# Experts of a MoE block: transposes and bias products gathered into two groups per expert

## The chip, the cores and the metric

The kernel runs on one core of a Trainium2 chip. The metric is the device time of one execution in microseconds (us). All times below are of that one core.

## The reference

A decoder block: an S5 branch and a gated MLP branch side by side, merged, then a mixture of 32 experts of which each token takes four, then a last norm. Only the mixture matters here (512 tokens of width 1024, float32):

```python
logits = tok @ router_w + router_b
top_val, top_idx = lax.top_k(logits, 4)
weights = jax.nn.softmax(top_val, axis=-1)
...
def expert_block(args):
    rows, e = args
    xb = tok[rows]
    gu = xb @ w_in[e] + b_in[e]                 # 1024 -> 2048
    gate, up = gu[:, :1024], gu[:, 1024:]
    gate = jnp.minimum(gate, 7.0)
    up = jnp.clip(up, -7.0, 7.0)
    act = (up + 1) * (gate * jax.nn.sigmoid(1.702 * gate))
    return act @ w_out[e] + b_out[e]            # 1024 -> 1024
...
out = zeros.at[row_tok].add(row_weight * expert rows)
```

## The kernel before, in words

The front part (the two branches, the router and the tables of tokens per expert) takes the first 430 us or so and is not changed. Then `expert` runs 32 times, unrolled, e0 to e31.

Every expert has a main part of up to 64 tokens. POOL gathers their rows into `xab[e % 3]`, two half rows to a partition, by an indirect DMA that is issued two experts ahead. Experts with more than 64 tokens run further blocks under `tc.If`: a `single` block (`c_up`, `c_down`; tiles `xc`, `actc`, `pc`) and a `pair` block (`ab_up`, `ab_out` with `pc` tiles). On this input 12 experts have the single block (e4, 6, 9, 12, 13, 16, 18, 22, 25, 27, 28, 30) and 6 the pair block (e11, 12, 17, 22, 26, 27); 17 have neither, and PE branches past the code of both. In the order of the program a single block stands under an If ahead of the main up (L1400), a pair block under one behind it (L1402), and their second halves under two Ifs behind the main up (L1411, L1413).

The weights stay in float32. SyncE (SP) loads them by `prefetch` as tiles of 1 MB, eight `wi` and four `wo` for an expert, into a ring of 19 tiles; a tile is asked for when the one that held its place has been read.

On the main path of an expert, PE (TensorE) does:

- two bias products into the PSUM tiles `pu` (`biased`, L1287): `sel` (which expert's bias goes to which row) times `bhl`;
- `ab_up` (L1293, products at L1300): 32 products, 8 K tiles by 2 halves u by 2 column groups g. K tiles 0 to 3 run for both halves, then 4 to 7 for u = 0, then 4 to 7 for u = 1. A product of float32 is two MATMUL instructions, so a K tile of one half is four in the profile, and a main up is 64;
- between those, after K tile 3, `start(e + 1)`: PE transposes the next expert's rows (`transposed`, L1264, into the PSUM tile `pt`), ACT moves them to SBUF scaled in eight pieces (L1270), DVE makes its `sel`;
- `swiglu` on each half `pu`: DVE g and u, ACT a sigmoid, DVE a product and `act` (L1278 to L1282);
- `ab_out` (L1312): transposes of `act` of half 0 (copied to `aab` by ACT at L1272), two bias products into `pd`, then `ab_down` (L1309), 16 products, four of them ahead of the transposes of half 1, twelve behind. DVE scales the result to `yab`, POOL adds it to the output by an indirect DMA.

PE's order is the order of the Python code (`tc.manual_schedule(engines={ET.PE})`); on DVE, ACT, POOL and SP a scheduler places the instructions. The pool of `pt` has two buffers; `pu` (two tiles) and `pd` have one each.

Of the kernel before, what the change touches and what calls it, by code (L numbers as in the profile page):

```python
# [9 lines left out]
F32 = mybir.dt.float32  # L10
# [18 lines left out]
NE, TOPK, DE = 32, 4, 1024  # L29
# [12 lines left out]
def tile_hybrid_block(ctx: ExitStack, tc: tile.TileContext, x, c, ada_w, ada_b, norm1_g, w_in,  # L42
# [20 lines left out]
    def H(shape, dt=F32, name="h"):  # L63
        return big.tile(shape, dt, tag="H", name=name)
# [63 lines left out]
    for i in range(2):  # L128
        t = H([128, 2, 1024], name="xt")
# [324 lines left out]
    pu = product(hT, True, evac_u, raw_in[0])  # L454
# [396 lines left out]
    aT = [(ahi[:, k], alo[:, k]) for k in range(4)]  # L851
# [62 lines left out]
    for i in range(2):  # L914
        t = H([128, 2, 1024], name="x2")
# [211 lines left out]
    xT, pps = {}, {}  # L1127
# [48 lines left out]
    tab0, tabp = [rt.tile([128, 1, 32, 3], I32, name=m) for m in ("tab0", "tabp")]  # L1176
# [44 lines left out]
    xab = [rt.tile([128, 512], F32, name=f"xab{a}") for a in range(3)]  # L1221
# [6 lines left out]
    pab = ctx.enter_context(tc.tile_pool(name="pab", bufs=1, space=PS, reuse_waits="tile"))  # L1228
# [22 lines left out]
    def gather_more(e):  # L1251

        x_ = xce[e % 3]
        with tc.If(single[e] > 0):
            gather(x_[:, 512:768], hrow4, tab1[:, 0, e, 0:1], 4)
        with tc.If(pair[e] > 0):
            gather(x_[:, 0:512], hrow2, tabp[:, 0, e, 0:1], 2)

    def transposed(src, n, tag, bufs, scaled=False):


        ps = PT()
# [12 lines left out]
    def swiglu(p, act):

        g, u, sg = [mo.tile([128, 256], F32, tag=t, bufs=1, name=t) for t in ("g", "u", "s")]
        v.tensor_scalar(g, p[:, 0:256], LIMIT, None, op0=OP.min)  # L1278
        sc.activation(sg, g, AF.Sigmoid, scale=ALPHA)  # L1279
        v.tensor_scalar(u, p[:, 256:512], -LIMIT, LIMIT, op0=OP.max, op1=OP.min)  # L1280
        v.tensor_mul(g, g, sg)
        v.scalar_tensor_tensor(act, u, 1.0, g, op0=OP.add, op1=OP.mult)  # L1282
        return act

    def biased(o, s_, n, cols_, first=True):

        return pe.matmul(o, s_, bhl[:, n, cols_], start=first, stop=False)  # L1287

    def acts(n, tag):
        return [mo.tile([128, 256], F32, tag=tag, bufs=n, name="act") for _ in range(n)]  # L1290


    def ab_up(xT, wi, sel, n, p, between=None):  # L1293
        for u in range(2):
            biased(p[u], sel[:, 1 + u], n, slice(0, 512))
        for k, u in [(k, u) for k in range(4) for u in range(2)] + [(k, u) for u in range(2) for k in range(4, 8)]:
            if between and (k, u) == (4, 0):
                between()
            for g in range(2):
                pe.matmul(p[u][64 * g:64 * g + 64, :].rearrange("p (a b) -> p a b", a=2),  # L1300
                          xT[:, k % 4, 64 * (k // 4):64 * (k // 4) + 64],
                          wi[k][:, :, 512 * g + 256 * u:512 * g + 256 * u + 256], start=False, stop=(k == 7))
        return p

    def ab_down(p, aT, j, wo, ks):

        for k in ks:
            for g in range(2):
                pe.matmul(p[64 * g:64 * g + 64, :], aT[:, k % 2, 16 * (k - k % 4):16 * (k - k % 4) + 64],  # L1309
                          wo[k // 2 + j][:, k % 2, 512 * g:512 * g + 512], start=False, stop=(j == 1 and k == 5))  # L1310

    def ab_out(pd, aT0, aT1, wo, sel, n, row):  # L1312
        for u in range(2):
            biased(pd[:, 256 * u:256 * u + 256], sel[:, 1 + u], n, slice(512, 768), u == 0)
        ab_down(pd, aT0, 0, wo, (0, 1))
        aT1 = aT1()
        ab_down(pd, aT0, 0, wo, (4, 5))
        ab_down(pd, aT1, 1, wo, (0, 1, 4, 5))
        y = mo.tile([128, 512], F32, tag="yab", bufs=2, name="yab")
        v.scalar_tensor_tensor(y, pd, row[:, 2:3].bitcast(F32), gate2h, op0=OP.mult, op1=OP.mult)  # L1320
        give(y, acc2, row[:, 1:2])


    def PC():
        return pcd.tile([128, 512], F32, tag="pc", name="pc")
# [27 lines left out]
    for t in xab[1:] + xce:  # L1353
        gp.memset(t, 0.0)

    def start(e):
        xT = transposed(xab[e % 3], 4, "xab", 2, True)
        sel = mo.tile([128, 3, 128], F32R, tag="sel", bufs=2, name="sel")
        v.tensor_scalar(sel, qsel, esel[:, e % 16:e % 16 + 1], None, op0=OP.mult)
        return xT, sel  # L1360

    def later_tables(ch):

        t = PT()
        if ch > 1:
            later_hots(ch)
        for i in range(4):
            spread(t, 128, i)
        s_ = start(0) if ch == 1 else None
        tab = mo.tile([128, 512], F32, tag="yab", bufs=2, name="tl")[:, 0:384].bitcast(I32) if ch > 1 else None  # L1370
        tab = tab.rearrange("p (n e w) -> p n e w", n=4, w=3) if ch > 1 else tab1
        tables(t, 128, rep32, tab, 4.0, 0, PT, mo_tile)
        if ch == 1:
            tables(t, 64, rep64, tabp, 2.0, 2, PT, mo_tile)
            v.copy_predicated(tab1[:, 0], pair4.unsqueeze(2).to_broadcast([128, 32, 3]), tab1[:, 2])
        gp.dma_start(tabl[4 * ch - 2:4 * ch + 2].rearrange("n p f -> p n f"), tab.rearrange("p n e w -> p n (e w)"))
        return s_

    ordered = tc.manual_schedule(engines={ET.PE})
    ordered.__enter__()  # L1380
    s_ = later_tables(1)
    most = nc.values_load(nbt[0:1, 96:97], min_val=0, max_val=NBMAX)
    with tc.If(most > 6):
        for ch in (2, 3, 4):
# [5 lines left out]
    nc.sync.dma_start(first, tab0[0:1].rearrange("p a e w -> p (a e w)"))  # L1390
    prefetch(24)

    def expert(e, xT, sel):
        (wi, wo), n = W[e], e // 16
        x_ = xce[e % 3]
        if e + 2 < NE:
            gather_first(e + 2)
            gather_more(e + 2)
        act, last = acts(2, "act"), acts(3, "actc")
        with tc.If(single[e] > 0):  # L1400
            c_up(transposed(x_[:, 512:768], 2, "xc", 2, True), wi, sel, n, last[2])
        with tc.If(pair[e] > 0):  # L1402
            p = ab_up(transposed(x_[:, 0:512], 4, "xab", 2, True), wi, sel, n, [PC(), PC()])
            for t, a_ in zip(p, last):
                swiglu(t, a_)
        nxt = []
        p = ab_up(xT, wi, sel, n, [pab.tile([128, 512], F32, tag=f"pu{u}", name="pu") for u in range(2)],
                  lambda: nxt.extend(start(e + 1) if e + 1 < NE else []))
        for t, a_ in zip(p, act):
            swiglu(t, a_)  # L1410
        with tc.If(single[e] > 0):  # L1411
            c_down(transposed(last[2], 2, "ac", 2), wo, sel, n, tab1[:, 0, e])
        with tc.If(pair[e] > 0):  # L1413
            lT = [transposed(t, 2, "ac", 2) for t in last[0:2]]
            ab_out(PC(), lT[0], lambda: lT[1], wo, sel, n, tabp[:, 0, e])
        aT0 = transposed(act[0], 2, "aab", 2)
        ab_out(pab.tile([128, 512], F32, tag="pd", name="pd"), aT0, lambda: transposed(act[1], 2, "aab", 2),
               wo, sel, n, tab0[:, 0, e])
        if e + 2 < NE:
            prefetch(12 * (e + 3))  # L1420
        return nxt

    for e in range(NE):
        s_ = expert(e, *s_)

# [118 lines left out]
```

## Time and profile before

| | |
|---|---|
| runs | 1573.04, 1579.26, 1576.98 us (median 1576.98) |
| profiled execution | 1574.68 us, of which the span is 1573.1 us |
| granted TensorE clock, mean | 0.962 |
| PE busy | 1405.7 us (89%) |
| DVE, ACT, POOL busy | 456.0, 345.4, 218.8 us |
| DMA | 497.09 MB, mean 316 GB/s over the span |
| main up products `pu<-wi,xab` | 2048 instructions, 464.5 us |
| main down products `pd<-wo,aab` | 1024 instructions, 233.9 us |
| single up, pair up (`pc<-wi,xc`, `pc<-wi,xab`) | 768 and 384 instructions, 88.5 and 83.7 us |

Busy time is counted over the whole span, front part included. PE's matrix instructions overlap, so a stretch of time on PE is best read as the distance between the starts of two rows. [...]

### The profile page before, as it was taken

To read this page: it belongs to the slowest core of one execution; us is meant where nothing else is said; L and a number is where in the kernel's file an instruction comes from. 1 tells how busy PE (TensorE), PEld (TensorE's weight loads), DVE (VectorE), ACT (ScalarE), POOL (GpSimd) and SP (SyncE) were. 2 spreads that over 40 slices of the span, in tenths; PEclk is the share of its full clock that TensorE was granted. 3 is DMA by queue.
4 is the path that set the end of the run, shared out by engine and by line. 5 is a ranking of instruction groups with operands and counts; after the bars stand their busy time and mean duration, and the time that the engine had idled before them with its cause. 6 is when DMAs were issued, how large, how long until landed. Compare 5 with 4: busy or idle time off the path is not lost.

```text
span 1573.1 us, 22103 instructions
## 1 busy us (share of the span) xinstructions
PE 1405.7 (89%) x7895; PEld 647.2 (41%) x7896; DVE 456.0 (29%) x1089; ACT 345.4 (22%) x831; POOL 218.8 (14%) x181
## 2 busy tenths in 40 slices
PE   5759999999588999979999889999999999998992
PEld 4548877777322333323333323333333333333330
DVE  7658932575321121111111111211111112111113
ACT  3453323334221121111111112111121111111112
POOL 3733100000201011102001111011101111011001
PEclk9879999999699999989999989999999999999996
DMA  9324686494799999999997999789999999679953
GB/s 313 124 67 141 204 273 184 139 375 158 269 397 408 403 407 408 397 410 406 410 361 263 362 397 407 293 331 400 406 405 367 397 409 400 243 266 342 380 187 129
DMA packets 128918, 497.09 MB, mean 316 GB/s; under 512 B 23589, under 2 KB 31237, under 8 KB 95973
## 3 DMA queue, kind: packets, MB, share of 16 engines
q1 hardware_dynamic: 113844, 468.50, 76.3%
q0 software_dynamic: 11888, 20.84, 5.9%
q10 hardware_dynamic: 3008, 5.38, 1.0%
q8 instruction: 113, 1.85, 0.5%
q14 instruction: 65, 0.52, 0.1%
HBM read 476.75 MB, written 20.40 MB: 316 GB/s over the span
## 4 chain that ended last, share of the span: by engine, by line
DMA 37%; issue 35%; PE 17%; DVE 3%; SPq 2%; ACT 1%; POOL 1%; another core or an unknown queue 1%; POOLq 1%; ACTq 0%; DVEq 0%
DMA acc<-yab,tab 16%; PE g L386 13%; DMA xab<-hrow,tab 11%; DMA acc<-yc,tab 6%; DMA acc<-yab,tabp 3%; PE m L386 1%; SPq L120 1%; PE m L343 1%; DMA acc<-x 1%; DVE st L186 1%; SPq L145 1%; POOL xab L1241 1%; SPq L149 1%; DVE ex L412 0%
## 5 line engine op out<-in xcount | busy, mean ns | idle before, releaser
L1300 PE MATMUL pu<-wi,xab 128*64 128x512 f32 x2048 | 464.5, 606 | 0.7 <-issue 0.7
L1300 PEld LDWEIGHTS pu<-wi,xab 128*64 128x64 f32 x2048 | 145.3, 139 | 282.5 <-issue 271.8
L1309 PE MATMUL pd<-wo,aab 128*64 128x512 f32 x1024 | 233.9, 599 | 7.5 <-ACT aab L1272 7.5
L1270 ACT ACTIVATE xab<-pt,sh2c,g2c 128x64 f32<-128x64 f32 x304 | 93.8, 414 | 369.6 <-PE pt L1264 369.6
L1278 DVE TENSOR_SCALAR g<-pu 128x256 f32<-128x256 f32 x64 | 27.1, 423 | 415.9 <-PE pu L1300 413.5
L1309 PEld LDWEIGHTS pd<-wo,aab 128*64 128x64 f32 x1024 | 67.9, 136 | 129.0 <-issue 111.3
L1349 POOL DMA_INDIRECT acc<-yab,tab x32 | 50.7, 1585 | 367.7 <-DVE yab L1320 282.5
L1332 PE MATMUL pc<-wi,xc 128*32 128x512 f32 x768 | 88.5, 609 | 9.4 <-DMA wi<-in_moe_w_in 6.6
L1241 POOL DMA_INDIRECT xab<-hrow,tab x32 | 33.8, 1057 | 375.1 <-PE pt L1264 372.7
L1279 ACT ACTIVATE s<-g 128x256 f32<-128x256 f32 x88 | 36.5, 415 | 221.5 <-DVE g L1278 219.7
L1300 PE MATMUL pc<-wi,xab 128*64 128x512 f32 x384 | 83.7, 594 | 1.0 <-ACT xab L1270 0.9
L1320 DVE SCALAR_TENSOR_TENSOR yab<-pd,tab,gate2h 128x512 f32<-128x512 f32 x32 | 24.0, 751 | 200.1 <-PE pd L1309 200.1
L1272 ACT ACTIVATE aab<-pt 128x256 f32<-128x256 f32 x64 | 24.5, 383 | 207.1 <-PE pt L1264 207.1
L174 ACT ACTIVATE whi<-wraw 128x1024 fp32r<-128x1024 f32 x46 | 48.1, 1056 | 88.0 <-PE g L386 63.6
L386 PE MATMUL g<-hhi,whi 128*128 128x512 f32 x160 | 65.3, 408 | 1.8 <-ACT hhi L498 1.8
L386 PE MATMUL g<-hlo,whi 128*128 128x512 f32 x160 | 64.4, 402 | 1.6 <-DVE hlo L492 1.4
L386 PE MATMUL g<-hhi,wlo 128*128 128x512 f32 x160 | 64.0, 400 | 0.0
L1278 DVE TENSOR_SCALAR g<-pc 128x256 f32<-128x256 f32 x24 | 10.2, 424 | 170.1 <-PE pc L1332 96.4
L1287 PE MATMUL pu<-bhl,sel 128*128 128x512 f32 x64 | 24.6, 467 | 36.8 <-PEq L1402 36.8
L175 POOL TENSOR_TENSOR wlo<-wraw,whi 128x1024 fp32r<-128x1024 f32 x16 | 40.6, 2544 | 89.9 <-ACT whi L174 89.5
L1264 PE MATMUL pt<-ident,act 128*128 128x128 f32 x176 | 36.4, 294 | 18.5 <-PEq L1413 9.6
L1264 PEld LDWEIGHTS pt<-ident,act 128*128 128x128 f32 x176 | 17.9, 141 | 81.4 <-issue 80.4
(443 smaller groups left out, 1611.2 us busy)
## 6 DMA issues: line engine op xcount, KB each, us to landing
wi<-in_moe_w_in SPq DMA_DIRECT2D x256, 1024.0 KB, 15.2
wo<-in_moe_w_out SPq DMA_DIRECT2D x128, 1024.0 KB, 12.9
adaw<-in_ada_w SPq DMA_DIRECT2D x16, 1024.0 KB, 5.5
wraw<-in_w_in SPq DMA_DIRECT2D x12, 1024.0 KB, 7.2
wraw<-in_ada_w SPq DMA_DIRECT2D x8, 1024.0 KB, 9.5
wraw<-in_w_out SPq DMA_DIRECT2D x4, 1024.0 KB, 9.9
xt<-in_x SPq DMA_DIRECT2D x4, 512.0 KB, 5.2
wraw<-in_w_in SPq DMA_DIRECT2D x4, 512.0 KB, 13.0
```

The source lines that it names most:

```text
L174: sc.activation(dst_hi, src, AF.Copy)
L175: lo.tensor_sub(dst_lo, src, dst_hi)
L386: pe.matmul(P["ps"][m], l, r, start=(k == 0 and n == 0), stop=(k == 2 * P["n"] - 1 and n == 2))
L1241: gp.indirect_dma_start(out=dst, out_offset=None, in_=rows_, in_offset=bass.IndirectOffsetOnAxis(ap=idx, axis=0), bounds_check=n * S - 1, ...
L1264: pe.transpose(ps[:, 128 * j:128 * j + 128], src[:, 128 * j:128 * j + 128], ident)
L1270: sc.activation(t[:, o:o + w], ps[:, o:o + w], AF.Identity, scale=g2c[:, k:k + 1], bias=sh2c[:, k:k + 1])
L1278: v.tensor_scalar(g, p[:, 0:256], LIMIT, None, op0=OP.min)
L1279: sc.activation(sg, g, AF.Sigmoid, scale=ALPHA)
L1300: pe.matmul(p[u][64 * g:64 * g + 64, :].rearrange("p (a b) -> p a b", a=2), xT[:, k % 4, 64 * (k // 4):64 * (k // 4) + 64], wi[k][:, :, 51 ...
L1309: pe.matmul(p[64 * g:64 * g + 64, :], aT[:, k % 2, 16 * (k - k % 4):16 * (k - k % 4) + 64], wo[k // 2 + j][:, k % 2, 512 * g:512 * g + 512 ...
L1332: pe.matmul(p[32 * g:32 * g + 32, :].rearrange("p (a b) -> p a b", a=2), xT[:, k % 2, 32 * (k // 2):32 * (k // 2) + 32], wi[k][:, :, 256 * ...
L1349: gp.indirect_dma_start(out=rows_, out_offset=bass.IndirectOffsetOnAxis(ap=icol, axis=0), in_=y, in_offset=None, compute_op=OP.add)
```

## The change

`start` is split into `rows_of` (the transposes of the next expert's rows) and `selectors` (its `sel`), and the bias products are taken out of `ab_up` and `ab_out` (`up_biases`, `out_biases`, `main_sums`). In the main path:

- the transposes of `act` of half 0 and the bias products of `pd` now stand ahead of the last K tile of half 1 of the up (`before_last`, at (k, u) = (7, 1)), with `swiglu` of half 0 asked for there;
- the transposes of `act` of half 1, those of the next expert's rows and the bias products of the next expert's `pu` now stand halfway through the down (`halfway`), eight products behind its start instead of four;
- nothing but the products stands at the start of the up or of the down; `sel` of the next expert is made early in the expert.

```diff
-    def ab_up(xT, wi, sel, n, p, between=None):
+    def up_biases(sel, n, p):
         for u in range(2):
             biased(p[u], sel[:, 1 + u], n, slice(0, 512))
+        return p
+
+    def ab_up(xT, wi, p, between=None):
...
-            if between and (k, u) == (4, 0):
+            if between and (k, u) == (7, 1):
                 between()
...
-    def ab_out(pd, aT0, aT1, wo, sel, n, row):
-        for u in range(2):
-            biased(pd[:, 256 * u:256 * u + 256], sel[:, 1 + u], n, slice(512, 768), u == 0)
-        ab_down(pd, aT0, 0, wo, (0, 1))
+    def ab_out(pd, aT0, aT1, wo, row):
+
+        ab_down(pd, aT0, 0, wo, (0, 1, 4, 5))
         aT1 = aT1()
-        ab_down(pd, aT0, 0, wo, (4, 5))
         ab_down(pd, aT1, 1, wo, (0, 1, 4, 5))
...
+    def rows_of(e):
+        return transposed(xab[e % 3], 4, "xab", 2, True)
+
+    def main_sums(e, sel):
+
+        return up_biases(sel, e // 16, [pab.tile([128, 512], F32, tag=f"pu{u}", name="pu") for u in range(2)])
...
+        sel1 = selectors(e + 1) if e + 1 < NE else None
...
+        aT, nxt = [], []
+
+        def before_last():
+            swiglu(p[0], act[0])
+            aT.append(transposed(act[0], 2, "aab", 2))
+            aT.append(out_biases(pab.tile([128, 512], F32, tag="pd", name="pd"), sel, n))
+
+        def halfway():
+            aT1 = transposed(act[1], 2, "aab", 2)
+            if sel1 is not None:
+                nxt.extend((rows_of(e + 1), sel1, main_sums(e + 1, sel1)))
+            return aT1
+
+        ab_up(xT, wi, p, before_last)
+        swiglu(p[1], act[1])
```

On PE, at the start of an expert and through its main up, before (`pu<-bhl,sel` are the bias products, `pt<-ident` transposes; a row of the program is one product, two instructions of the profile where it is float32):

```order
L1402 UNCONDITIONAL_BRANCH x2
L1287 MATMUL pu<-bhl,sel 128x512 x2
L1300 MATMUL pu<-wi,xab 64x512 x16
L1264 MATMUL pt<-ident,xab_3335 128x128 x4
L1300 MATMUL pu<-wi,xab 64x512 x16
L1411 COMPARE_AND_BRANCH
```

The same place in the changed program:

```order
L1416 UNCONDITIONAL_BRANCH x2
L1304 MATMUL pu<-wi,xab 64x512 x30
L1264 MATMUL pt<-ident,act 128x128 x2
L1287 MATMUL pd<-bhl,sel 128x256 x2
L1304 MATMUL pu<-wi,xab 64x512 x2
L1437 COMPARE_AND_BRANCH
```

The bias products of `pu` and the transposes of `xab` have left the up, and the transposes of `act` with the bias products of `pd` stand in it, two products ahead of its end.

On PE, behind the Ifs, the main down of the same expert before:

```order
L1413 UNCONDITIONAL_BRANCH x2
L1264 MATMUL pt<-ident,act 128x128 x2
L1287 MATMUL pd<-bhl,sel 128x256 x2
L1309 MATMUL pd<-wo,aab 64x512 x4
L1264 MATMUL pt<-ident,act 128x128 x2
L1309 MATMUL pd<-wo,aab 64x512 x12
```

And in the changed program:

```order
L1439 UNCONDITIONAL_BRANCH x2
L1317 MATMUL pd<-wo,aab 64x512 x8
L1264 MATMUL pt<-ident,act 128x128 x2
L1264 MATMUL pt<-ident,xab_3335 128x128 x4
L1287 MATMUL pu<-bhl,sel 128x512 x2
L1317 MATMUL pd<-wo,aab 64x512 x8
```

One group of eight matrix rows halfway down stands in place of two groups, one ahead of the first product and one after four.

The third place is the start of the main up of e1 with the waits of its rows (DMAHW is a load that has to have landed, Activation is ACT), before:

```order
L1287 MATMUL pu<-bhl,sel 128x512 x2
L1300 MATMUL pu<-wi,xab 64x512 [waits DMAHW7_49]
L1300 MATMUL pu<-wi,xab 64x512 x3
L1300 MATMUL pu<-wi,xab 64x512 [waits DMAHW1_49]
L1300 MATMUL pu<-wi,xab 64x512 x3
```

And in the changed program:

```order
L1304 MATMUL pu<-wi,xab 64x512 [waits DMAHW7_49,Activation_49]
L1304 MATMUL pu<-wi,xab 64x512 x3
L1304 MATMUL pu<-wi,xab 64x512 [waits DMAHW1_49,Activation_49]
L1304 MATMUL pu<-wi,xab 64x512 x3
L1304 MATMUL pu<-wi,xab 64x512 [waits DMAHW3_49,Activation_49]
```

The products of the up now wait for ACT as well as for their weight tile. A row with two waits takes one more instruction on PE; with all its rows, branches and waits PE's program has 29,188 instructions before, 749 for each expert, and 758 or 759 for each expert after the change.

## Rows read from the trace of the kernel before

**Rows 1.** Windows: us, busy (x) of PE, PEld, DVE, ACT, POOL; PEclk, DMA, GB/s
```profile
430.00:702.00 272.00, 245.18 (x1289) 82.90 (x1285) 43.64 (x100) 46.77 (x138) 31.34 (x24) 0.98 1.02 404
702.00:1546.00 844.00, 797.90 (x4405) 277.46 (x4401) 142.83 (x332) 141.80 (x432) 94.74 (x71) 0.99 0.91 349
```
**Rows 2.** Timeline of PE in e9, its single block up
```profile
689.39 1.06 PE L1332 MATMUL pc<-wi,xc 128*32 128x512 f32 x8 [1.39 <-DMA wi<-in_moe_w_in]
700.56 1.93 PE L1332 MATMUL pc<-wi,xc 128*32 128x512 f32 x8 [0.58 <-DMA wi<-in_moe_w_in]
```
**Rows 3.** Timeline of PE, e20 (neither block) and the start of e21
```profile
1110.28 0.70 PE L1287 MATMUL pu<-bhl,sel 128*128 128x512 f32 x2 [0.58 <-PEq L1402]
1110.91 7.09 PE L1300 MATMUL pu<-wi,xab 128*64 128x512 f32 x32
1117.93 0.66 PE L1264 MATMUL pt<-ident,xab 128*128 128x128 f32 x4
1118.52 7.09 PE L1300 MATMUL pu<-wi,xab 128*64 128x512 f32 x32
1126.60 0.41 PE L1264 MATMUL pt<-ident,act 128*128 128x128 f32 x2 [1.00 <-DVE u L1280]
1126.77 0.48 PE L1287 MATMUL pd<-bhl,sel 128*128 128x256 f32 x2
1127.48 1.94 PE L1309 MATMUL pd<-wo,aab 128*64 128x512 f32 x8 [0.23 <-ACT aab L1272]
1129.35 0.44 PE L1264 MATMUL pt<-ident,act 128*128 128x128 f32 x2
1129.72 5.37 PE L1309 MATMUL pd<-wo,aab 128*64 128x512 f32 x24
1135.72 0.70 PE L1287 MATMUL pu<-bhl,sel 128*128 128x512 f32 x2 [0.62 <-PEq L1402]
```
**Rows 4.** Waits of PE, 430 to 1550 us: tile, line, releaser: sum us, count, longest
```profile
PE pu L1287 <- PEq L1402: 29.3, 25, 3.9
PE pd L1309 <- ACT aab L1272: 7.5, 32, 0.2
```
**Rows 5.** Timeline of PE, behind the Ifs: e25 (single block) and e26 (pair block)
```profile
1298.70 0.41 PE L1264 MATMUL pt<-ident,act 128*128 128x128 f32 x2 [0.33 <-PEq L1413]
...
1349.49 0.41 PE L1264 MATMUL pt<-ident,act 128*128 128x128 f32 x2 [0.20 <-DVE act L1282]
```
**Rows 6.** Timeline of DVE, e20, half 0: first and last step
```profile
1122.22 0.42 DVE L1278 TENSOR_SCALAR g<-pu 128x256 f32<-128x256 f32 x1 [11.72 <-PE pu L1300]
1123.65 0.42 DVE L1282 SCALAR_TENSOR_TENSOR act<-u,g 128x256 f32<-128x256 f32 x1
```
**Rows 7.** The page's costliest groups: busy us, mean ns of one, idle before, releaser
```profile
L1270 ACT ACTIVATE xab<-pt,sh2c,g2c 128x64 f32<-128x64 f32 x304 | 93.8, 414 | 369.6 <-PE pt L1264 369.6
```
**Rows 8.** Timeline of PE: starts of e1, e16, e29, and e29's first products
```profile
453.34 0.70 PE L1287 MATMUL pu<-bhl,sel 128*128 128x512 f32 x2 [3.18 <-PEq L1402]
...
971.22 0.70 PE L1287 MATMUL pu<-bhl,sel 128*128 128x512 f32 x2 [1.64 <-PEq L1402]
...
1456.73 1.19 PE L1287 MATMUL pu<-bhl,sel 128*128 128x512 f32 x2 [3.88 <-PEq L1402]
1457.85 5.41 PE L1300 MATMUL pu<-wi,xab 128*64 128x512 f32 x14
```
**Rows 9.** Windows, as rows 1, of e29's start
```profile
1456.00:1463.00 7.00, 6.27 (x16) 2.09 (x18) 0.00 (x0) 0.00 (x0) 0.00 (x0) 0.55 0.93 321
```
**Rows 10.** The page's DMA queues: kind, packets, MB, share of 16 engines
```profile
q8 instruction: 113, 1.85, 0.5%
```
**Rows 11.** DMA queues from 900 to 906 us, e14's start
```profile
q8 instruction: 1, 0.02, 1.0%
```
**Rows 12.** Windows, as rows 1, of 100 us
```profile
1100.00:1200.00 100.00, 94.31 (x470) 31.85 (x472) 17.97 (x42) 18.12 (x56) 9.99 (x8) 1.00 1.02 408
```
**Rows 13.** Windows, as rows 1, from e20's last up product to its down
```profile
1125.40:1127.50 2.10, 0.87 (x8) 0.49 (x6) 0.97 (x3) 0.45 (x2) 0.00 (x0) 1.00 1.03 433
```

More of the change, by code (lines that the diff above doesn't have):

```diff
@@ L1302, in ab_up, with out_biases @@
                           wi[k][:, :, 512 * g + 256 * u:512 * g + 256 * u + 256], start=False, stop=(k == 7))
-        return p
+    def out_biases(pd, sel, n):
+        for u in range(2):
+            biased(pd[:, 256 * u:256 * u + 256], sel[:, 1 + u], n, slice(512, 768), u == 0)
+        return pd
     def ab_down(p, aT, j, wo, ks):
@@ L1354, in tile_hybrid_block, with selectors @@
         gp.memset(t, 0.0)
-    def start(e):
-        xT = transposed(xab[e % 3], 4, "xab", 2, True)
+    def selectors(e):
         sel = mo.tile([128, 3, 128], F32R, tag="sel", bufs=2, name="sel")
         v.tensor_scalar(sel, qsel, esel[:, e % 16:e % 16 + 1], None, op0=OP.mult)
-        return xT, sel
+        return sel
+    def rows_of(e):
+        return transposed(xab[e % 3], 4, "xab", 2, True)
+    def main_sums(e, sel):
+        return up_biases(sel, e // 16, [pab.tile([128, 512], F32, tag=f"pu{u}", name="pu") for u in range(2)])
     def later_tables(ch):
@@ L1368, in later_tables @@
             spread(t, 128, i)
-        s_ = start(0) if ch == 1 else None
+        s_ = rows_of(0) if ch == 1 else None
         tab = mo.tile([128, 512], F32, tag="yab", bufs=2, name="tl")[:, 0:384].bitcast(I32) if ch > 1 else None
@@ L1380, in tile_hybrid_block @@
     ordered.__enter__()
-    s_ = later_tables(1)
+    xT0 = later_tables(1)
+    sel0 = selectors(0)
     most = nc.values_load(nbt[0:1, 96:97], min_val=0, max_val=NBMAX)
@@ L1391, in tile_hybrid_block, with expert @@
     prefetch(24)
-    def expert(e, xT, sel):
+    def expert(e, xT, sel, p):
         (wi, wo), n = W[e], e // 16
@@ L1402, in expert @@
         with tc.If(pair[e] > 0):
-            p = ab_up(transposed(x_[:, 0:512], 4, "xab", 2, True), wi, sel, n, [PC(), PC()])
-            for t, a_ in zip(p, last):
+            pp = [PC(), PC()]
+            xp = transposed(x_[:, 0:512], 4, "xab", 2, True)
+            ab_up(xp, wi, up_biases(sel, n, pp))
+            for t, a_ in zip(pp, last):
                 swiglu(t, a_)
[L1406 to L1410, printed above, removed]
+        aT, nxt = [], []
[10 more added lines that the diff above has]
+        swiglu(p[1], act[1])
         with tc.If(single[e] > 0):
@@ L1414, in expert @@
             lT = [transposed(t, 2, "ac", 2) for t in last[0:2]]
[L1415 to L1418, printed above, removed]
+            ab_out(out_biases(PC(), sel, n), lT[0], lambda: lT[1], wo, tabp[:, 0, e])
+        ab_out(aT[1], aT[0], halfway, wo, tab0[:, 0, e])
         if e + 2 < NE:
@@ L1421, in expert @@
         return nxt
+    s_ = xT0, sel0, main_sums(0, sel0)
     for e in range(NE):
```

## The prediction, as put on record before the run

> **What bounds the kernel now.** I read the windows first, since the shares over the whole span mix stages. The mixture has two parts [rows 1]. From 430 to 702 us the DMA share is 1.02 at 404 GB/s, so the loads run flat out, and PE waits for weight tiles in e9 [rows 2]: its products stand at 689.39 and 700.56 us, about 11 us apart, where the first group of eight ran for 1.06 us. What PE gains ahead of that point it waits off there. From 702 to 1546 us PE is busy 797.9 of 844 us and the DMA share is 0.91: PE is the bound. So the change is priced over e10 to e31 and the second half of e9, some 22.5 experts: 10 with neither block, 6.5 with a single alone, 6 with a pair.
>
> The timeline of e20 shows what an expert without blocks costs PE [rows 3]. It takes 1135.72 − 1110.28 = 25.44 us. Thirty-two product instructions take 1117.93 − 1110.91 = 7.02 us and eight take 1129.35 − 1127.48 = 1.87; the difference over 24 gives 0.2146 us each, and 0.15 us for getting into a stretch. The 96 of up and down take 20.60 us, so 4.84 us are not products.
>
> **The change part by part.** Of these 4.84 us, between starts of rows 3: bias of `pu` 0.63, transposes of `xab` 0.59, transposes of `act` 0 with bias of `pd` 0.88, transposes of `act` 1 0.37, and 0.15 for each of the two stretches that these cut in the middle. Sum 2.77. The remainder is PE's stall at two branches, 0.85 and 1.2 with the drain of the last product.
>
> A group that comes back to float32 products pays a return: two transposes alone take 0.17 (1126.60 to 1126.77), but 0.37 when products follow, so 0.20. Before there are four returns, after it two. Group one becomes 0.15 + 0.17 + 0.48 = 0.80 (the return is in the 0.48), group two 0.15 + 0.17 + 0.39 (0.59 less a return) + 0.63 = 1.34. Sum 2.14. The groups save 2.77 − 2.14 = 0.63 us: two returns, and the 0.23 us that the first down product waited for ACT's copy to `aab`. That wait stands in every expert, 7.5 us over 32 [rows 4]; now the four instructions of the last K tile (0.86 us) and the branch stall lie over the copy.
>
> In an expert without blocks the transposes of `act` 0 also wait 1.00 us behind the branch for DVE [rows 3], where a branch behind which nothing is late costs 0.62 there and 0.33 in e25 [rows 5]. The down now begins with products whose operand is long ready, so 0.2 may go too, up to 0.4. I take 0.7 for an expert with neither block (0.5 to 0.95), 0.6 for a single alone (0.4 to 0.7), 0.8 for a pair, where the transposes of `act` 1 wait 0.20 more for DVE in e26 [rows 5] (0.5 to 1.0). Sum: 10 × 0.7 + 6.5 × 0.6 + 6 × 0.8 = **15.7 us**, bounds 11 to 20.
>
> What covers the new waits. Group one needs `act` 0. Half 0 of `pu` ends 16 instructions into the second half of the up, at 1118.52 + 3.43 = 1121.95; DVE's last step for it ends at 1123.65 + 0.42 = 1124.07 [rows 6], 2.12 us later. PE gets to group one after three K tiles, 12 × 0.2146 + 0.15 = 2.73 us. That leaves **0.6 us**, the narrowest margin. If the cover is gone, everything on PE queues behind these transposes. Group two needs `act` 1, some 2.1 us after the up, and comes a branch stall and 16 product instructions (0.6 to 1.0 + 3.4 us) later: a margin of about 2 us. The next expert's rows are scaled behind group two by eight ACT pieces of 0.41 us [rows 7], 3.3 us end to end; the bias of `pu`, 16 down instructions and the branch (0.6 + 3.4 + 0.6) lie over those. The gathers are issued two experts ahead and the loads are asked for behind the same reads as before, so POOL's and SP's queues keep their order.
>
> The product rows that now wait for ACT as well as their load cost one extra instruction each on PE. Between rows that take 0.21 us I price those at nothing; at 0.05 us each, the upper end I allow, nine make 0.45 us an expert and take 10 us back. A dispatch that runs ahead of 0.2146 us products, as the uniform 7.02 and 1.87 show, speaks for nothing.
>
> **The stall at an expert's first branch.** Waits on PE's own sequencer at L1402 sum to 29.3 us in 25 cases [rows 4], mostly 0.6, but e1, e2, e14, e15 and e29 stand 3.2 to 3.9 , e16 and e28 1.6 to 1.7 (of each kind the first, and e29, in [rows 8]). [...]
>
> I read these as instruction fetch. The queue of instructions moves 113 packets, 1.85 MB [rows 10], one of them during e14's stall [rows 11]. PE's program has 29,188 instructions, so a packet is 258, near enough 256. An expert is 749 long, 768 − 19: its first branch moves back 19 in a block from one expert to the next and returns after 256/19 = 13.5 experts, which is the distance of the long stalls. In the changed program an expert is 758.6, so it moves back 9.4 and returns after 27. Laid out from the same start, the bad places come at e1 to e3, hidden ahead of e9's wait for loads, and at e28 to e30. There e28 and e29 have theirs before too, and e30, which has a single block and so the shorter jump, gets one like e16's, +1.3. What goes is e14 at 4.2 (2.8 and half of the clock's 2.7, as an estimate between none and all), e15 at 5.6 and e16 at 1.4. I take −4.2 − 5.6 − 1.4 + 1.3 = **−9.9 us**, bounds −14 to +4 (the places rest on my counting; a long stall on one more expert is +3 to +6). [...]
>
> **The loads as a cap.** The share of 0.91 is a mean: from 1100 to 1200 us it is 1.02 at 408 GB/s [rows 12], as flat out as ahead of e9. A faster PE comes there earlier, and what about four experts save in such a stretch (4 × 0.7 = 2.8 us) may be waited off for weight tiles. I add **+2 us** (0 to 8, where ten experts lose their saving).
>
> Sum: 1574.7 − 15.7 − 9.9 + 2 = 1551.1 us against the profiled execution's own time, which is 2.3 below the median of the runs. Between 1551.1 and 1553.4 I say **1552 us**.
>
> **The rivals.**
>
> *The groups save, the stalls don't move away* (they fall on other plain experts between e10 and e31). For: the places rest on a count of instructions, and one expert off matters. Against: the 13.5 fits three returns. 1574.7 − 15.7 + 2 is 1561, and with a long stall more up to 1567; with the runs' 2.3 I say 1564.
>
> *The loads or the extra wait rows eat it.* For: e9, and the share of 1.02. Against: 0.91 over the stretch. 15.7 less 10 for the rows, or less 8 for loads, and no gain from stalls: 1567 to 1571, with both 1577.
>
> *Slower: group one waits for `act` 0.* One mechanism, ahead of the last K tile. Its margin is 0.6 us where DVE and ACT are free. If `act` 0 comes later by t (DVE also makes `sel`, and the blocks' halves run on it), each expert pays t − 0.6. It decides from t = 0.6 + 25/22.5 = 1.7 us on; at 2.2 us late, 22.5 × 1.6 = 36, and 1587. DVE is busy 142.8 of 844 us [rows 1], which speaks against.
>
> [...]
>
> **How the numbers follow.** Chances: the forecast 0.58, stalls elsewhere 0.22, loads or wait rows 0.14, group one waits 0.04, the clock 0.02. The likeliest's own range is 1543 (bounds of both gains) to 1560. Of all cases it reaches to the stalls' rival: 1540 to 1569 leaves out some 0.2. Half a per cent, 7.9 us, is what a measurement here tells from no change: faster is below 1569, all of the first case, nearly all of the second and a fifth of the third, 0.82; same 0.13; slower 0.05.
>
> **What would show it.** Right: e20's period falls from 25.4 to about 24.7 us; no wait for ACT at the first down product; group one starts with no wait for DVE; L1416's waits have no 3 us case in e14 to e16 and one at e29; the windows from 702 us show about 25 us less. Wrong: a wait for DVE or ACT ahead of the last K tile, a long stall in e17 to e27, or PE waiting for `wi` from e20 on.

## The result, and the profile after

The changed kernel took 1556.38 us (median of four runs, 1551.44 to 1557.99) against 1575.71 us for the kernel before: a ratio of 0.9867, 95% interval 0.9843 to 0.9891. It is faster by 1.3%, and the forecast was 1552 us. The profiled execution took 1551.44 us where that of before took 1574.68, 23.2 us less. It is the fastest of the four, so the medians, 19.3 us apart, are the better measure of the gain.

The windows of the changed kernel, with the columns of [rows 1]: first up to e9's main part, then to PE's last product.

```profile
430.00:699.00 269.00, 239.96 (x1277) 90.22 (x1273) 42.71 (x100) 46.28 (x137) 31.42 (x24) 0.97 1.02 404
699.00:1523.00 824.00, 782.45 (x4403) 294.79 (x4399) 142.06 (x332) 142.90 (x432) 95.58 (x71) 1.00 0.92 358
```

The stretch that [rows 1] has at 844 us is 824 us now. The loads ahead of e9 run at the 404 GB/s of before, and PE, busy 782 of the 824 us, is still the bound behind it.

The timeline of PE through e20, and the start of e21, which answers to [rows 3]:

```profile
1092.18 13.10 PE L1304 MATMUL pu<-wi,xab 128*64 128x512 f32 x60 [0.95 <-PEq L1416]
1105.21 0.44 PE L1264 MATMUL pt<-ident,act 128*128 128x128 f32 x2
1105.40 0.48 PE L1287 MATMUL pd<-bhl,sel 128*128 128x256 f32 x2
1105.82 1.08 PE L1304 MATMUL pu<-wi,xab 128*64 128x512 f32 x4
1107.62 3.65 PE L1317 MATMUL pd<-wo,aab 128*64 128x512 f32 x16 [0.73 <-PEq L1439]
1111.21 0.44 PE L1264 MATMUL pt<-ident,act 128*128 128x128 f32 x2
1111.48 0.60 PE L1264 MATMUL pt<-ident,xab 128*128 128x128 f32 x4
1111.84 0.72 PE L1287 MATMUL pu<-bhl,sel 128*128 128x512 f32 x2
1112.49 3.65 PE L1317 MATMUL pd<-wo,aab 128*64 128x512 f32 x16
...
1117.49 1.08 PE L1304 MATMUL pu<-wi,xab 128*64 128x512 f32 x4 [1.34 <-PEq L1416]
```

Both groups stand as the order has them, and neither waits. Group one takes 1105.82 − 1105.21 = 0.61 us and group two 1112.49 − 1111.21 = 1.28; the four pieces of before, without the 0.15 us of getting into each stretch, took 0.63 + 0.59 + 0.88 + 0.37 = 2.47. That is 0.58 us saved, with the 0.23 us of the wait for ACT's copy among them. Yet the expert takes 1117.49 − 1092.18 = 25.31 us, against 25.44. What was saved, and the 0.27 us that the down comes sooner behind its branches (a gap of 0.73 for 1.00), is lost again at the right edge of the last row: the gap at the next expert's first branch is 1.34 us in e21, where [rows 3] has 0.62 (in e20 it is 0.95 for 0.58). 0.58 + 0.27 − 0.72 is the 0.13 us that is left.

The starts of six experts on PE (e2, e14, e15, e28, e29, e31), which answer to [rows 8]:

```profile
482.27 14.79 PE L1304 MATMUL pu<-wi,xab 128*64 128x512 f32 x60 [4.35 <-PEq L1416]
...
896.37 13.10 PE L1304 MATMUL pu<-wi,xab 128*64 128x512 f32 x60 [0.73 <-PEq L1416]
...
921.32 13.10 PE L1304 MATMUL pu<-wi,xab 128*64 128x512 f32 x60 [0.87 <-PEq L1416]
...
1402.76 13.10 PE L1304 MATMUL pu<-wi,xab 128*64 128x512 f32 x60 [2.75 <-PEq L1416]
...
1435.03 14.79 PE L1304 MATMUL pu<-wi,xab 128*64 128x512 f32 x60 [4.22 <-PEq L1416]
...
1498.73 13.10 PE L1304 MATMUL pu<-wi,xab 128*64 128x512 f32 x60 [0.84 <-PEq L1416]
```

The long stalls of e14 and e15 (3.33 and 3.46 us before) are gone; e28 and e29 have theirs, and e2's of 4.35 lies ahead of e9. Behind the stall of e29 the same 60 product instructions take 14.79 us in place of 13.10: the granted clock is 0.76 from 1435 to 1442 us and 1.00 in the 7 us behind that.

DVE in the same e20, the last step for `act` 0, then the next expert's `sel`, which runs right ahead of the steps for `act` 1, and the last of those; they answer to [rows 6]:

```profile
1104.18 0.42 DVE L1282 SCALAR_TENSOR_TENSOR act<-u,g 128x256 f32<-128x256 f32 x1
1107.46 0.42 DVE L1364 TENSOR_SCALAR sel<-qsel,esel 128x384 fp32r<-128x384 f32 x1 [2.85 <-PEq L1439]
...
1109.22 0.42 DVE L1282 SCALAR_TENSOR_TENSOR act<-u,g 128x256 f32<-128x256 f32 x1
```

`act` 0 is ready at 1104.60 and group one reads it at 1105.21: a margin of 0.61 us. `act` 1 is ready at 1109.64, 1.57 us ahead of group two.

### The profile page after: what moved, and what is told of

It is laid out like the page before. It is cut to its first block, busy times and chain, and to the rows that moved or that the text cites. A ratio compares the mean times of both kernels' runs of the same rounds, so it can differ in the third digit from the quotient of the medians.

```text
span 1549.9 us, 22296 instructions
## 1 busy us (share of the span) xinstructions
PE 1388.0 (90%) x7895; PEld 673.5 (43%) x7896; DVE 451.5 (29%) x1089; ACT 346.1 (22%) x830; POOL 220.4 (14%) x181
## 5 line engine op out<-in xcount | busy, mean ns | idle before, releaser
L1304 PEld LDWEIGHTS pu<-wi,xab 128*64 128x64 f32 x2048 | 165.1, 139 | 315.3 <-issue 304.5
L1317 PEld LDWEIGHTS pd<-wo,aab 128*64 128x64 f32 x1024 | 74.5, 137 | 155.8 <-issue 141.3
L1338 PE MATMUL pc<-wi,xc 128*32 128x512 f32 x768 | 85.1, 594 | 3.1 <-ACT xc L1270 2.9
L1355 POOL DMA_INDIRECT acc<-yc,tab x12 | 19.9, 1657 | 350.8 <-DVEq L1439 232.8
L1278 DVE TENSOR_SCALAR g<-pc 128x256 f32<-128x256 f32 x24 | 10.2, 424 | 162.4 <-PE pc L1338 86.7
L1304 PEld LDWEIGHTS pc<-wi,xab 128*64 128x64 f32 x384 | 27.3, 137 | 56.2 <-issue 50.9
L1338 PEld LDWEIGHTS pc<-wi,xc 128*32 128x32 f32 x768 | 23.6, 110 | 57.4 <-issue 40.1
```

The lines of the kernel that those rows point to most:

```text
L1338: pe.matmul(p[32 * g:32 * g + 32, :].rearrange("p (a b) -> p a b", a=2), xT[:, k % 2, 32 * (k // 2):32 * (k // 2) + 32], wi[k][:, :, 256 * ...
L1355: gp.indirect_dma_start(out=rows_, out_offset=bass.IndirectOffsetOnAxis(ap=icol, axis=0), in_=y, in_offset=None, compute_op=OP.add)
```

## The experiments

To tell the stalls from the groups, no-ops of PE were put between the products of the main up. A no-op moves all instructions behind it, and so the **place** of an expert's first branch in its stretch of 256 of PE's instructions (0 to 255, counted in the program). The common edit, with the numbers of the first kernel below:

```diff
+PAD_FIRST = 154
+PAD = (18, 21, 21, 19, 19, 20, 19, 20, 19, 19, 19, 19, 18, 18, 18, 18,
...
+        n_pad = PADS[0].pop(0) if between else 0
+        for i, (k, u) in enumerate(steps):
+            for _ in range(n_pad // 16 + (i < n_pad % 16)):
+                pe.nop(hint="pad", nofuse=True)
...
+    for _ in range(PAD_FIRST):
+        pe.nop(hint="pad", nofuse=True)
```

The 256 is an estimate: in the kernel before the long stalls return after 13 or 14 experts of 749 instructions (e1 and e2, e14 and e15, e28 and e29), and 749 is three times 256 less 19, a 13.5th of it. The packets of the instruction queue agree: the first kernel below has 29,932 instructions, 744 more than the kernel before, and 116 packets in place of 113 [rows 10], 258 instructions a packet in both.

The stretch that the readings use is from the first row behind e10's Ifs to the first behind e31's, 21 experts. It is 1521.41 − 732.95 = 788.46 us before and 1498.73 − 728.32 = 770.41 us in the changed kernel, 18.1 less. The rows before are

```profile
732.95 0.70 PE L1287 MATMUL pu<-bhl,sel 128*128 128x512 f32 x2 [0.80 <-PEq L1402]
...
1521.41 0.70 PE L1287 MATMUL pu<-bhl,sel 128*128 128x512 f32 x2 [0.57 <-PEq L1402]
```

and, in the changed kernel, the row of e31 above and this one of e10:

```profile
728.32 13.10 PE L1304 MATMUL pu<-wi,xab 128*64 128x512 f32 x60 [0.73 <-PEq L1416]
```

A stretch is read from one execution, and waits for weight tiles differ a little from one to the next: `a_const` and `a_same` below have the same instructions at the same places from e1 on, and 3.8 us between them. Ratios are against the kernel before, in runs on the same chip.

| kernel | ratio (95%) | median us | e10 to e31, us | e20, us |
|---|---|---|---|---|
| changed kernel | 0.9867 (0.9843 to 0.9891) | 1556.38 | 770.41 | 25.31 |
| before, place 100 (b_const) | 0.9951 (0.9929 to 0.9972) | 1569.73 | 770.30 | 25.34 |
| before, places of the changed kernel (b_slide) | 0.9937 (0.9916 to 0.9958) | 1568.18 | 776.71 | 25.35 |
| changed, place 100 (a_const) | 0.9886 (0.9849 to 0.9923) | 1559.50 | 763.96 | 24.96 |
| changed, all places 120 further (a_shift) | 0.9981 (0.9959 to 1.0003) | 1575.50 | 775.77 | 25.67 |
| changed, place 100, none ahead of e0 (a_same) | 0.9806 (0.9770 to 0.9841) | 1549.47 | 760.13 | 24.97 |
| group one alone, place 100 (g1_same) | 0.9934 (0.9910 to 0.9957) | 1569.33 | 779.93 | 25.26 |
| the same, act 1 behind eight (g1_late) | 0.9922 (0.9894 to 0.9949) | 1566.86 | 775.93 | 25.54 |
| group two alone, place 100 (g2_same) | 0.9826 (0.9780 to 0.9871) | 1552.92 | 765.28 | 25.09 |
| changed, pu's biases at the start (a_bias) | 0.9842 (0.9796 to 0.9888) | 1557.48 | 766.66 | 25.03 |
| changed, group one a K tile sooner (a_early) | 0.9873 (0.9812 to 0.9933) | 1560.32 | 767.26 | 25.34 |
| changed, place 172 (a_bad) | 1.0269 (1.0190 to 1.0348) | 1622.66 | 811.05 | 29.98 |
| changed, place 245 (a_245) | 0.9826 (0.9751 to 0.9900) | 1552.58 | 764.16 | 25.30 |

**The places alone: b_const, b_slide.** In `b_slide` the common edit has these numbers:

```diff
+PAD_FIRST = 4
+PAD = (255, 9, 9, 8, 8, 9, 9, 10, 9, 9, 9, 9, 9, 9, 9, 9,
...
```

> The kernel before, with no-ops of PE spread over the main up (18 to 24 per expert, 154 once ahead of e0), so that every expert's first branch stands at place 100 of its 256 instructions; nothing else is changed. Theory P (the long stalls at an expert's first branch go by that place): all of them go. After e9 that is e14 2.7, e15 2.9 and about 2.7 for the clock, e16 1.5, e28 1.5, e29 3.3 and 2.7, some 17 us: 1557 to 1561 against 1575.7 of before. Rival (the stalls come with time or with the state of the loads, not with the place): e14, e15 and e29 keep stalls of over 3 us, 1572 to 1580, and the no-ops may only add to it.

> The kernel before with some 9 no-ops per expert, so that each expert's first branch stands at the very place that it has in the changed kernel (206, 187, 175 ... 161, 147). Theory P: no long stall at e14 to e16; long ones at e2 and e3, hidden ahead of e9's wait, a half one at e4, e28 and e30, a long one at e29 as before; 9 to 11 us less than before, 1564 to 1568. Rival: as before, 1574 to 1578, with stalls at e14 and e15.

The starts of e14, e15 and e29 in `b_const`:

```profile
915.21 0.70 PE L1291 MATMUL pu<-bhl,sel 128*128 128x512 f32 x2 [0.58 <-PEq L1410]
...
940.56 0.70 PE L1291 MATMUL pu<-bhl,sel 128*128 128x512 f32 x2 [0.58 <-PEq L1410]
...
1454.14 0.70 PE L1291 MATMUL pu<-bhl,sel 128*128 128x512 f32 x2 [0.58 <-PEq L1410]
```

And of e3, e14 and e29 in `b_slide`:

```profile
522.46 1.19 PE L1291 MATMUL pu<-bhl,sel 128*128 128x512 f32 x2 [3.10 <-PEq L1410]
...
908.68 0.70 PE L1291 MATMUL pu<-bhl,sel 128*128 128x512 f32 x2 [0.58 <-PEq L1410]
...
1452.57 0.70 PE L1291 MATMUL pu<-bhl,sel 128*128 128x512 f32 x2 [3.67 <-PEq L1410]
```

With one place for all, every gap from e1 on is 0.58 us or less. With the changed kernel's places, the kernel before has its long stalls where the changed kernel has them: e3 now has one of 3.10 us where it had 0.58, e14 0.58 where it had 3.33. The stretch falls by 788.46 − 770.30 = 18.2 us in `b_const` and by 788.46 − 776.71 = 11.8 in `b_slide`. The total of `b_const` was missed: its 154 no-ops ahead of e0, where no product covers them, lengthened e0's first wait from 7.53 to 16.64 us, e10 starts 13.0 us later than before (745.99 for 732.95), and that reached the end.

**The changed kernel at other places: a_const, a_shift, a_same.** The numbers of `a_const`; `a_shift` has `PAD_FIRST = 120` and no other no-op, `a_same` has `PAD_FIRST = 0` and 169 in e0's up instead of 19:

```diff
+PAD_FIRST = 150
+PAD = (19, 12, 12, 11, 11, 11, 10, 10, 10, 10, 10, 10, 9, 9, 9, 9,
...
```

> The changed kernel with no-ops in the same way, every first branch at place 100. Theory P: the stalls of e28 (2.4 over the usual), e29 (3.5 and 2 to 2.7 for the clock), e30 (0.9) go, and so do the small excesses at e18 to e24 (0.2 to 0.6 each, 2.5 together), 11 to 12 us: 1544 to 1547. Against the kernel before with its first branches at the same place this is then the groups alone, 10 to 14 us. Rival (places do nothing, the change's 19 us are all the groups'): 1555 to 1558, and 19 us below its counterpart.

> The changed kernel with 120 no-ops once, ahead of e0, so that all its first branches stand 120 further (e13 181, e14 172, e15 163, e16 154, e17 145; e28 to e31 48 to 11). Theory P: stalls of over 3 us at e14 and e15, half ones at e13 and e16, none at e1 to e3 and none at e28 to e30: some 9 us come back at the end and 13 to 16 are paid in the middle, 1558 to 1564, and e0 to e3 hidden. Rival: the trace stays as it is but for 120 no-ops at the start, 1555 to 1558, stalls at e28 and e29.

> The changed kernel with every first branch from e1 on at place 100, as in the run with no-ops ahead of e0, but with those 150 put between e0's products instead, so that e0 starts as in the changed kernel. Theory P: e0 starts at about 420 us and not at 437; nothing over 0.9 us stands at a first branch after e1; e10 to e30 take 764 to 766 us (770.3 in the changed kernel), so 1546 to 1552 us. Rival (what the places give is waited off for loads elsewhere): waits for weight tiles after e9 of 8 us or more, 1553 to 1558.

The starts of e14, e15 and e29 in `a_shift`:

```profile
914.47 15.55 PE L1312 MATMUL pu<-wi,xab 128*64 128x512 f32 x60 [4.30 <-PEq L1424]
...
945.33 15.48 PE L1312 MATMUL pu<-wi,xab 128*64 128x512 f32 x60 [4.45 <-PEq L1424]
...
1456.41 13.10 PE L1312 MATMUL pu<-wi,xab 128*64 128x512 f32 x60 [0.92 <-PEq L1424]
```

120 no-ops, none of them after e0, carry the stalls from e28 and e29 (2.75 and 4.22 us in the changed kernel) to e14 and e15 (4.30 and 4.45). The totals of `a_const` and `a_shift` were missed, again by the no-ops ahead of e0: e0's products wait 12.36 and 9.97 us where the changed kernel's waited 3.05. In the stretch `a_const` also waits 2.11 us for a tile in the single up ahead of e22's main part, where `a_same` waits 0.72. `a_same` shows the changed kernel without no-ops ahead of e0, at 1549.47 us: the stretch is 770.41 − 760.13 = 10.3 us shorter than the changed kernel's, and it beats both kernels. Its e10 starts 8.9 us later than the changed kernel's (737.26 for 728.32), so the profiled executions are 1.4 us apart, and the medians 6.9.

**The groups one by one, at place 100: g1_same, g2_same, g1_late.** In `g1_same` the kernel before gets only this, with the biases taken out of `ab_out`:

```diff
-            if between and (k, u) == (4, 0):
-                between()
+            if between and (k, u) in ((4, 0), (7, 1)):
+                between(k)
...
+                swiglu(p[0], act[0])
+                aT.append(transposed(act[0], 2, "aab", 2))
+                aT.append(out_biases(pab.tile([128, 512], F32, tag="pd", name="pd"), sel, n))
```

`g1_late` adds the changed kernel's `ab_down(pd, aT0, 0, wo, (0, 1, 4, 5))` ahead of `aT1()`. `g2_same` is the changed kernel with this:

```diff
-        ab_up(xT, wi, p, before_last)
-        swiglu(p[1], act[1])
+        ab_up(xT, wi, p, lambda: None)
+        for t, a_ in zip(p, act):
+            swiglu(t, a_)
...
+        aT.append(transposed(act[0], 2, "aab", 2))
+        aT.append(out_biases(pab.tile([128, 512], F32, tag="pd", name="pd"), sel, n))
+        ab_out(aT[1], aT[0], halfway, wo, tab0[:, 0, e])
```

> Group one alone, every first branch from e1 on at place 100: act 0's transposes and pd's biases stand ahead of the last K tile, all else as in the kernel before (biases of pu at the expert's start, rows' transposes after K tile 3, transposes of act 1 after four down products). At the same place an expert with neither block takes 25.34 us in the kernel before and 24.96 in the changed one. Theory X (the returns saved by group two are nearly taken by a longer gap at the expert's start, 0.80 for 0.58): group one alone gives 25.05 to 25.15, the better part of the 0.38. Rival Y (each group gives its share as in the prediction, the copy's 0.23 to one and two returns to two, and the gap is a loss of neither): 25.10 to 25.20 for this one and as much from the other. Rival Z (group one only moves the wait: act 0 is late ahead of the last K tile): 25.3 or more, with waits for DVE or ACT in the up.

> Group two alone, every first branch from e1 on at place 100: transposes of act 1, of the next rows and the biases of the next pu halfway down; act 0's transposes and pd's biases stay ahead of the down. Theory X: the gap at the expert's start is 0.80 in place of 0.58 here too, and an expert with neither block takes 25.20 to 25.30 us (25.34 before). Rival Y: 25.10 to 25.20. Rival Z (group one gives nothing, so this gives all): 24.95 to 25.0.

> Group one alone as before, first branches at place 100, but the transposes of act 1 stand behind eight down products as in the changed kernel, not behind four. Theory (group one alone lost in experts with a block, 37.42 us for a single where the kernel before has 36.74, since its down begins sooner and act 1 is then late behind four products, 15.6 us of waits for DVE in all): the waits for DVE's act go to below 3 us, an expert with a single takes 36.5 to 36.7, one with neither 25.1 to 25.2. Rival (DVE is late by the order of its work in those kernels, not by the four products): the single stays above 37.2 and the waits above 10 us.

Waits of PE in `g1_same` from 730 us on (sum, count, longest), and in `g1_late`:

```profile
PE pt L1268 <- DVE act L1286: 15.6, 22, 1.6
```

```profile
PE pd L1317 <- ACT aab L1276: 9.9, 21, 0.5
```

And e19's down in `g1_late`:

```profile
1098.35 3.65 PE L1317 MATMUL pd<-wo,aab 128*64 128x512 f32 x16 [0.72 <-PEq L1431]
1101.94 0.44 PE L1268 MATMUL pt<-ident,act 128*128 128x128 f32 x2
1102.85 3.65 PE L1317 MATMUL pd<-wo,aab 128*64 128x512 f32 x16 [0.47 <-ACT aab L1276]
```

Group one alone is a loss: 779.93 against `b_const`'s 770.30, 9.6 us. None of the three theories gave that. The loss lies in the experts with a block (e11 takes 56.41 us for 55.37, e13 29.92 for 29.23), while e20 gains 0.08. The down now begins sooner, so `act` 1 is late behind its first four products. Moving those transposes back behind eight takes that wait away, as expected, but not the loss, which is still 5.6 us: the products behind them need ACT's copy at once and wait 0.47 us for it in each expert. An expert without blocks was to take 25.1 to 25.2 us there, and e20 takes 25.54. Group two alone gains 770.30 − 765.28 = 5.0 us, and e20 lies at 25.09, below the range of theory X. Both together gain 770.30 − 760.13 = 10.2. So the transposes of the next rows and the biases of `pu` are what covers `act` 1's copy in group two. The changed kernel's own last expert, which has no next rows, shows the same wait, at its second half of the down:

```profile
1518.66 3.65 PE L1317 MATMUL pd<-wo,aab 128*64 128x512 f32 x16 [0.47 <-ACT aab L1272]
```

**What stands first behind the branch: a_bias.**

```diff
-                nxt.extend((rows_of(e + 1), sel1, main_sums(e + 1, sel1)))
+                nxt.extend((rows_of(e + 1), sel1))
...
+        p.extend(main_sums(e, sel))
         ab_up(xT, wi, p, before_last)
```

> The changed kernel, first branches at place 100, but the biases of pu at the expert's own start again (behind the branch, as in the kernel before) and not in group two. Theory X (the gap grew because a float32 product and no longer the bias stands first behind the branch): the gap is 0.58 again, and as group two then needs a return of its own (0.2) the expert takes 24.9 to 25.0 us, no more and no less than the changed kernel's 24.96. Rival (the gap grew for another reason, a wait of the rows or the no-ops): it stays at 0.80, and the expert takes 25.15 us.

The start of its e20, and then that of e20 in `a_same`:

```profile
1101.43 0.70 PE L1291 MATMUL pu<-bhl,sel 128*128 128x512 f32 x2 [0.58 <-PEq L1424]
```

```profile
1098.50 13.10 PE L1312 MATMUL pu<-wi,xab 128*64 128x512 f32 x60 [0.80 <-PEq L1422]
```

The gap is 0.58 us with the bias first and 0.80 with the product first, at the same place. The expert is not shorter for it (25.03 against 24.97), because group two then pays a return without the bias in it. The stretch is 6.5 us longer than that of `a_same`: 2.8 of these lie between the starts of e21 and e22, where a single's up waits 1.99 us for a weight tile; the rest was not taken apart.

**The margin of group one: a_early.** 

```diff
-            if between and (k, u) == (7, 1):
+            if between and (k, u) == (6, 1):
```

> The changed kernel, first branches at place 100, group one two K tiles ahead of the end instead of one. Theory (the prediction's margin of 0.6 us between act 0 and group one): these transposes come 0.86 us sooner, wait about 0.25 us for DVE's act in each expert, and an expert with neither block takes 25.1 to 25.25 us (24.96 at one K tile). Rival (act 0 is ready well before): no wait, 24.93 to 24.98.

Group one of its e20:

```profile
1116.21 0.41 PE L1268 MATMUL pt<-ident,act 128*128 128x128 f32 x2 [0.33 <-DVEq L1445]
```

It waits, 0.33 us, and the expert is 0.37 longer than in `a_same`: all of the gain of both groups. The 0.86 us by which it came sooner less 0.33 leaves 0.53 us of margin at the change's own place.

**The dose: a_bad, a_245.** As `a_same`, with the no-ops of e0's up changed (`a_bad`; `a_245` has 58):

```diff
-PAD = (169, 12, 12, 11, 11, 11, 10, 10, 10, 10, 10, 10, 9, 9, 9, 9,
+PAD = (241, 12, 12, 11, 11, 11, 10, 10, 10, 10, 10, 10, 9, 9, 9, 9,
```

> The changed kernel with every first branch from e1 on at place 172. Theory P: each expert with neither block has a stall of 3.5 to 4.5 us there and, where the clock falls behind it, up to 2.5 more, so 28 to 31 us in place of 24.96; a single alone one to 2.5 us; experts with a pair, which don't skip it, none. e10 to e30 then take 810 to 830 us (760.2 at place 100), with 10 to 20 us more ahead of e9: 1605 to 1640 us. Rival (the stalls fall where several things meet, not on one place): fewer than half of the ten show one, below 1580.

> The changed kernel with every first branch from e1 on at place 245, where e21 stood in the changed kernel with a gap of 1.34 us in place of 0.80. Theory P: the small excesses go by the place as well; all experts with neither block have a gap of 1.2 to 1.4 and take 25.3 to 25.5 us, e10 to e30 764 to 768: 1552 to 1558. Rival (1.34 was the state of the loads at that time): gaps of 0.7 to 0.9, 1547 to 1552.

The start of e20 in `a_bad`, and below it the instruction queue in the 5.6 us around that wait, 1144.4 to 1150 us (packets, MB, share):

```profile
1149.96 14.81 PE L1312 MATMUL pu<-wi,xab 128*64 128x512 f32 x60 [5.51 <-PEq L1424]
```

```profile
q8 instruction: 1, 0.02, 1.2%
```

Those of e15 and e20 in `a_245`:

```profile
928.45 13.10 PE L1312 MATMUL pu<-wi,xab 128*64 128x512 f32 x60 [1.37 <-PEq L1424]
...
1098.86 13.10 PE L1312 MATMUL pu<-wi,xab 128*64 128x512 f32 x60 [1.47 <-PEq L1424]
```

At place 172 all nine experts with neither block from e10 to e29 have a wait of 4.1 us or more (e31 has none, 0.95), and the stretch is 811.05 − 760.13 = 50.9 us longer. The profile puts eight of the nine down to PE's sequencer, and e23's to a weight tile. In the windows of five of them (e15, e19, e20, e21 and e24) one instruction packet comes; in `a_same`, in the 4.6 us around e20's start (1094 to 1098.6), none does. So the long stall goes with an instruction packet at that point. At place 245 the same nine have 1.0 to 2.0, more spread than the 1.2 to 1.4 that was expected, and the stretch is 4.0 us longer.

## Why the prediction was right

**What bounds the kernel.** Right behind e9. Ahead of it the forecast had no gain, and e10's first product starts at 728.32 where it was 732.95 + 0.63 = 733.58: 5.3 us sooner. 2.7 of these stand already at e0's first product (421.74 for 424.40), and 1.3 of the 2.7 at a product of the front part, which the change does not touch (412.96 for 414.28). e0's biases now run ahead of its branches; that they give the other 1.4 is not shown, and the rest was not taken apart.

**The groups.** The mechanism was right, the size too large: 15.7 us was forecast over 22.5 experts, 14.7 over the 21 of the stretch (9 × 0.7 + 6 × 0.6 + 6 × 0.8). At one place they give 10.2 (`b_const` to `a_same`), at the changed kernel's own places 776.71 − 770.41 = 6.3. e20's period, which was to fall to 24.7 us, is 25.31, and 24.97 at place 100. Of the 10.2, the six experts with a pair give 4.7, as forecast; the six with a single alone give 2.7 in place of 3.6, and the nine with neither 2.8 in place of 6.3. The term of the pieces themselves was right: 0.63 us by the sum, 0.58 in e20's rows. What was mis-sized is the gap at an expert's start, which the sum left at 0.85: with a product first it is 0.22 longer at the same place, which with the drain below makes 0.58 + 0.01 − 0.22 = 0.37 an expert without blocks in place of 0.7, and the changed kernel's places add up to 0.5 in e19 to e24. These, and longer stalls at the end than `b_slide` has at the same places (4.22 for 3.67 in e29), are why the groups give less there than at place 100. The drain behind the up, priced at 0.2, gives 0.27 in e20 (0.73 for 1.00), but 0.01 at place 100, where it is 0.94 for 0.95.

**The stalls.** Right in that the place sets them, in where they fall and nearly in size: −9.9 us forecast, 11.8 measured by `b_slide`. e14 to e16 lost theirs; e2, e3, e28 and e29 have theirs, as laid out. The starts of e14 and e15 before, and the rows that end their first 32 product instructions, show what the terms 4.2 and 5.6 were worth:

```profile
904.71 0.70 PE L1287 MATMUL pu<-bhl,sel 128*128 128x512 f32 x2 [3.33 <-PEq L1402]
905.34 8.79 PE L1300 MATMUL pu<-wi,xab 128*64 128x512 f32 x32
914.05 0.66 PE L1264 MATMUL pt<-ident,xab 128*128 128x128 f32 x4
...
934.41 1.19 PE L1287 MATMUL pu<-bhl,sel 128*128 128x512 f32 x2 [3.46 <-PEq L1402]
935.53 9.31 PE L1300 MATMUL pu<-wi,xab 128*64 128x512 f32 x32
944.77 0.66 PE L1264 MATMUL pt<-ident,xab 128*128 128x128 f32 x4
```

Over e20's gap of 0.58, the waits are 2.75 and 2.88 us. Over e20's 7.02 us [rows 3] the products take 914.05 − 905.34 − 7.02 = 1.69 and 944.77 − 935.53 − 7.02 = 2.22 us more, and e15's bias 0.49 more, at a granted clock of 0.76 from 903 to 910 us and 0.66 from 931 to 938. That is 4.4 and 5.6 us, with 1.7 and 2.7 of them behind the wait, where the sum had half of 2.7 and 2.7. Its 2.7 is e29's: 14 products take 5.41 us where 14 × 0.2146 + 0.15 is 3.15, and the bias 1.19 for 0.70 [rows 8], at a granted clock of 0.55 [rows 9]. That the stalls are a fetch of instructions was the author's reading; the runs show a packet of the instruction queue in e14's [rows 11] and in five of `a_bad`, and not what PE waits for.

**Loads, margins, clock.** +2 us was put for the loads: behind e9 PE waits 1.3 us for a weight tile in e11, and 0.94 in e15, which is hardly more than the gap that stands there anyway. Group one's margin was worked out at 0.6 us and is 0.61 in the rows; group two's of about 2 is 1.57. The extra wait of the product rows, priced at nothing between products, costs nothing there: 60 product instructions take 1105.21 − 1092.18 = 13.03 us, which is 60 × 0.2146 + 0.15. The clock does not fall in group two; the window 1111.2 to 1112.5 us of the changed kernel:

```profile
1111.20:1112.50 1.30, 1.30 (x12) 0.92 (x10) 0.00 (x0) 0.76 (x3) 0.14 (x1) 1.00 1.03 422
```

So of the 23.2 us of the profiled executions, 11.8 are stalls that moved, about 6.3 the groups, 4.6 lie ahead of e10's first row (728.32 for 732.95) and 0.5 behind e31's. The profiled execution came out at the 1551.1 us of the sum because a gain that was not forecast, ahead of e10, made up for the groups: that is luck. By the medians the gain is 19.3 us where 25 was forecast. Of the rivals, the stalls that don't move away fell with `b_slide`, the wait of group one with the 0.61 us, and a fall of the clock in group two, given 0.02, with the window's 1.00 (before, 1.00 in [rows 13]).

## What to carry to other kernels

A change that adds or removes a few instructions per step in an unrolled program with branches can gain or lose more by where the branches fall than by what it does (here 11.8 us of stalls against about 6.3 of the groups): compare the two versions with their branches at the same place before crediting the edit. When fill work is gathered, look for which piece covers which copy: half of this regrouping was slower than none (group one alone, by 9.6 us over 21 experts). The gap behind the branch depended on what stood first there (0.58 us with the bias, 0.80 with a product), so moving the first instruction elsewhere wasn't free.

## What the runs showed of the hardware

- **The place decides the stall.** The first row behind both Ifs stands 298 to 303 instructions behind an expert's first branch. Counted in the programs of before, `b_slide`, `a_shift`, `a_bad` and the change, experts with neither block had 3.1 us or more whenever that row stood at 205 to 234 of its 256 (one exception of 31: e31 of `a_bad`, 0.95), and once at 255 (e10 of `a_shift`, 3.66, which the profile puts down to a weight tile); at 193 or less they had between 0.57 and 1.34 us. In `a_245`, where it stands at 32 to 36, they had 0.96 to 2.14. So the bad landing is near the end of the 256. The branch and the landing keep their distance in all these kernels, so whether the place of the one or of the other counts is not shown. One instruction packet comes in each of five long waits of `a_bad`. It isn't the distance of the jump that counts here: at places 100 and 172 both jumps have the same length, and one costs 0.80 us and the other 4.1 to 5.5. Nor does a landing further on cost more: at 172 it lies in the 256 behind the branch's own (172 + 303 is under 512), at 245 two on (245 + 298 is over), and there the wait is the shorter one, 1.0 to 2.0 us. Why the last part of the 256 is the bad one is not shown.
- **A no-op is cheap between products and dear ahead of e0.** 154 of them in a row ahead of e0 cost 16.64 − 7.53 = 9.1 us, 0.06 us each; 18 spread between the products of e19 leave it at 25.35 us in `b_const`, as it is before without them.
- **The stall's price has two parts here.** In `a_bad` e20 waits 5.51 us, and the 60 product instructions behind it take 14.81 us in place of 13.10, with a granted clock of 0.75 from 1150 to 1157 us and of 1.00 behind that.
